# RWKV-7 recurrence hops: the old state is decayed and added on VectorE in place of identity matmuls, and each hop's output products stand behind the next hop's first products

## The chip, the cores and the metric

The kernel runs on one core of one Trainium2 chip. TensorE multiplies 128x128 tiles into PSUM, VectorE and ScalarE work on SBUF and PSUM, GpSimd (POOL) on SBUF; SyncE issues most of the transfers. The metric is the device time of one execution in microseconds, lower is better.

## The reference, cut to what matters

One layer of a bidirectional RWKV-7 / neighbourhood-attention network over 512 sample tokens and 128 prompt tokens, width 1024. The change lies in the RWKV branch, which has 8 heads of 64 channels and runs one recurrence forward and one backward:

```python
def _wkv_step(s, inp):
    r, w, k, v, a, b = inp
    sa = jnp.einsum("bhvk,bhk->bhv", s, a)
    s = s * w[:, :, None, :] + sa[..., None] * b[:, :, None, :] + v[..., None] * k[:, :, None, :]
    return s, jnp.einsum("bhvk,bhk->bhv", s, r)
...
    s_f, y_f = _wkv_scan(s0[:, 0], rh, _heads(decay[:, :, 0]), _heads(k_dir[:, :, 0]), vh,
                         -kk, kk * _heads(iclr[:, :, 0]), False)
    s_b, y_b = _wkv_scan(s0[:, 1], rh, _heads(decay[:, :, 1]), _heads(k_dir[:, :, 1]), vh,
                         -kk, kk * _heads(iclr[:, :, 1]), True)
    y = y_f + y_b
```

Around it stand the input projection, a gated merge with the attention branch, and a feed-forward block. The sample starts from a given state, the prompt from zero, and the prompt's last state is an output.

## The kernel before, in words

All is in fp32; the wide projections split each operand into a high and a low fp32r part and multiply three times (helpers at L223, L311 and L1856).

The recurrence is computed in chunks of 64 tokens. The sample gives eight chunks (slots `sl` 0 to 7), the prompt two (slots 8 and 9). Two heads, h = 0 and 1, share a tile of 128 partitions, one in each half, so four tiles `ct` are worked through one after the other. For each tile, `main` and `inv` form all products inside the chunks (tiles `AG`, `TG`, `R_`, `Rt`), and `carry` then hops from chunk to chunk with the state. A *line* `l` is a slot in one direction; a hop takes the forward and the backward line of a slot, so four products (two lines, two heads) make a group. Hops 0 and 1 also take the prompt's slots, and their groups have eight.

`ZV` holds for each line and head the incoming state in the head's own half of the partitions and the values in the other half. A hop `s` in the program's order:

1. First products (L1393), `AG` by `ZV`, into PSUM; ScalarE copies them to `x0` (L1396).
2. Identity products (L1405): the old state is multiplied by an identity matrix into the PSUM tile `pn`, so that the new state can be accumulated onto it. Not for slot 7, which has no successor, nor for slot 8, whose state is zero.
3. Old-state output products (L1411), `ZV` by `R_`, into the output tile `Y`.
4. Second products (L1420), `Rt` by `x0`; ScalarE writes them into `ZV` over the old state (L1426).
5. State products (L1433), `TG` by `ZV`, onto `pn`; VectorE multiplies `pn` by the decay `Dt` into the state half of the next line of `ZV` (L1445, one instruction for each head and both lines), or into `zf` for the prompt's last state (L1439).
6. Output products (L1450), `ZV` by `TG`, into `Y`.

After the last hop ScalarE copies `Y` out (L1455); the prompt's output is copied after hop 1 (L1453).

The order on TensorE, VectorE, ScalarE and POOL is that in which the program is written (`tc.manual_schedule`). `carry` is a generator that yields after the steps 1 to 3, after step 4 and after step 6. At each yield `weave` puts other work in: filler matmuls of the wide projections (L223), in a number from the table `plan`, and pieces of another generator. In carries 0 to 2 that one is the preparation of the next tile (L645 to L751, with a scan on VectorE at L696, the activations L650 to L721 on ScalarE, and `last`, which forms the next `AG` at L1168 and `R_` at L1171 on VectorE; the next tile's first matmuls are L1189). In carry 3 it is the gating of the merged outputs (L1554, L1556 and L1579 on VectorE, L195 splitting weights). After step 6 the plan has mostly six fillers in carries 0 to 2 and four in carry 3. The preparation of a scale (L682, L684), the elementwise steps L723 to L742 and the chunk inverse (L1310, L1317) appear in the profile too.

## Time and profile before

| | |
|---|---|
| median of 3 runs | 1151.46 us (1148.97 to 1151.8) |
| the profiled execution | 1151.04 us, of which the span is 1149.3 us |
| granted TensorE clock | 0.995 |
| busy: TensorE, VectorE, ScalarE, POOL | 97%, 68%, 46%, 17% of the span |
| first products (L1393) of the four carries | 298.9 to 627.1 us from the span's start |
| TensorE waiting at L1393 for VectorE's L1445 | 0.7 us, 3 times |

Times in the profile are microseconds from the start of the span. A matmul in fp32 is recorded as two instructions, so a count of x8 in the trace is four products of the program. Durations of matmuls overlap; what one costs TensorE is seen from the distance between starts. In brackets behind a row stands how long the engine was idle before it and what ended that.

### The profile page before, as it was taken

The numbers are of one execution on the slowest core, as the hardware profiler recorded it, in microseconds if no ns is written. First come the engines' busy times: TensorE is split into PE (matmuls) and PEld (weight loads), VectorE is DVE, ScalarE is ACT, GpSimd is POOL, SyncE is SP. The second block draws the span as 40 slices with busy tenths as digits, with TensorE's granted clock in tenths as the row PEclk, the third lists the DMA queues.
The fourth block names the chain that finished last, engine by engine and source line by source line (L and its number), as shares of the span: only waits on it lengthen the run. The fifth ranks groups of instructions, "written<-read, shape, count | busy, mean of one in ns | idle before, by whom it ended". The sixth has DMA issues, their size and how long they took to land.

```text
span 1149.3 us, 26860 instructions
## 1 busy us (share of the span) xinstructions
PE 1117.0 (97%) x11160; PEld 990.9 (86%) x11160; DVE 777.8 (68%) x1641; ACT 533.7 (46%) x1052; POOL 195.1 (17%) x262
## 2 busy tenths in 40 slices
PE   6999999999999999999999999999999999999998
PEld 4688878799888888888898788999899989998997
DVE  4565465769558847936787846897478747874775
ACT  4444576665465665456443524654134413441340
POOL 1163244321101212120100421110101010101000
PEclk8999999999999999999999999999999999999999
DMA  9752677654433533343743872222212221232122
GB/s 340 261 113 91 199 277 236 198 153 125 107 75 86 148 85 93 96 119 86 254 122 105 265 213 72 92 93 93 91 56 92 94 90 55 92 97 88 55 91 94
DMA packets 60482, 149.16 MB, mean 130 GB/s; under 512 B 7460, under 2 KB 22436, under 8 KB 60360
## 3 DMA queue, kind: packets, MB, share of 16 engines
q1 hardware_dynamic: 54888, 131.16, 34.7%
q0 software_dynamic: 4032, 14.68, 6.5%
q10 hardware_dynamic: 1440, 1.59, 0.5%
q8 instruction: 88, 1.44, 0.5%
q14 instruction: 34, 0.28, 0.1%
HBM read 118.41 MB, written 14.32 MB: 115 GB/s over the span
## 4 chain that ended last, share of the span: by engine, by line
PE 74%; DVE 10%; issue 8%; ACT 4%; DMA 2%; POOL 1%; SPq 0%; ACTq 0%; DVEq 0%; POOLq 0%
PE acc L311 24%; PE f L1856 21%; PE fl L223 8%; PE mm L223 5%; PE psa L1044 1%; PE lg L959 1%; PE pt L988 1%; DVE RL L1321 1%; DVE pr L1317 1%; PE po L1006 1%; PE w L1420 1%; PE w L1393 1%; DMA o<-o_d 1%; PE w L1433 1%; DMA wlo<-wst 1%
## 5 line engine op out<-in xcount | busy, mean ns | idle before, releaser
L1856 PE MATMUL f<-t,whi 128*128 128x320 f32 x640 | 141.7, 310 | 0.2
L311 PE MATMUL acc<-whi,u 128*128 128x512 f32 (+1 forms) x448 | 136.1, 386 | 0.0
L1856 PE MATMUL f<-b,whi 128*128 128x320 f32 x608 | 135.0, 310 | 0.4 <-DVE b L212 0.4
L223 PE MATMUL fl<-h,whi 128*128 128x320 f32 x672 | 121.4, 321 | 0.0
L1856 PEld LDWEIGHTS f<-t,whi 128*128 128x128 f32 x640 | 106.8, 188 | 0.8 <-issue 0.4
L223 PEld LDWEIGHTS fl<-h,whi 128*128 128x128 f32 x672 | 102.1, 189 | 4.6
L192 ACT CAST whi<-wst 128x1024 fp32r<-128x1024 f32 (+1 forms) x77 | 79.3, 1033 | 52.2 <-PE acc L311 41.5
L1856 PEld LDWEIGHTS f<-b,whi 128*128 128x128 f32 x608 | 101.7, 188 | 1.1 <-issue 0.6
L1856 PE MATMUL f<-t,wlo 128*128 128x320 f32 x320 | 98.9, 309 | 0.0
L311 PEld LDWEIGHTS acc<-whi,u 128*128 128x128 f32 x448 | 83.5, 188 | 16.6
L1856 PE MATMUL f<-b,wlo 128*128 128x320 f32 x304 | 94.1, 309 | 0.0
L1909 ACT CAST whi<-ws 128x1024 fp32r<-128x1024 f32 x40 | 42.0, 1051 | 104.5 <-PE f L1856 45.6
L311 PE MATMUL acc<-wlo,u 128*128 128x512 f32 (+1 forms) x224 | 86.3, 385 | 0.0
L1923 POOL TENSOR_TENSOR ws<-wst 128x512 f32<-128x512 f32 x20 | 29.1, 1454 | 334.7 <-DVE wlo L1912 226.3
L195 DVE TENSOR_TENSOR wlo<-wst,whi 128x1024 fp32r<-128x1024 f32 (+2 forms) x57 | 60.1, 1066 | 30.6 <-ACT whi L192 30.0
L311 PE MATMUL acc<-whi,h 128*128 128x512 f32 x240 | 79.2, 404 | 0.8 <-DVE h L436 0.8
L1724 DVE SCALAR_TENSOR_TENSOR tt<-acc,G 128x512 f32<-128x512 f32 (+1 forms) x51 | 34.7, 680 | 59.0 <-PE acc L311 45.4
L223 PE MATMUL fl<-h,wlo 128*128 128x320 f32 x336 | 63.8, 322 | 0.0
L1909 ACT CAST whi<-wst 128x1024 fp32r<-128x1024 f32 (+1 forms) x48 | 41.3, 869 | 42.3 <-PE acc L311 25.1
L1856 PEld LDWEIGHTS f<-t,wlo 128*128 128x128 f32 x320 | 60.1, 188 | 0.0
L1912 DVE TENSOR_TENSOR wlo<-ws,whi 128x1024 fp32r<-128x1024 f32 x40 | 55.4, 1386 | 5.4 <-ACT whi L1909 5.4
L1445 DVE TENSOR_TENSOR ZV<-w,Dt 64x128 f32<-64x128 f32 x64 | 18.4, 288 | 58.5 <-PE w L1433 57.4
(342 smaller groups left out, 2533.2 us busy)
## 6 DMA issues: line engine op xcount, KB each, us to landing
wst<-in_w_dram SPq DMA_DIRECT2D x66, 512.0 KB
wst<-in_w_rw_dram SPq DMA_DIRECT2D x31, 512.0 KB
wlo<-wst POOLq DMA_DIRECT2D x28, 512.0 KB, 4.7
wa<-in_w_ada_dram SPq DMA_DIRECT2D x24, 512.0 KB
f<-in_w_ada_dram SPq DMA_DIRECT2D x16, 512.0 KB
wst<-in_w_qkv_dram SPq DMA_DIRECT2D x12, 512.0 KB
o<-o_d SPq DMA_DIRECT2D x14, 320.0 KB
x<-in_xs_dram SPq DMA_DIRECT2D x8, 512.0 KB
```

The source lines that it names most:

```text
L192: act.copy(hi[:, :n], st[:, :n])
L195: dve.tensor_tensor(out=lo[:, a:b], in0=st[:, a:b], in1=hi[:, a:b].bitcast(F32), op=ALU.subtract)
L223: pe.matmul(ps[:, :t1 - t0], w[:, a:a + 128], x[:, k0 + kt, t0:t1], start=n == 0, stop=n == 3 * nk - 1)
L311: pe.matmul(pss[i][:, a:b], lhs(x, kt, ts_), w[:, cs_], start=ki == 0 and n == 0, stop=ki == last and n == 2)
L959: pe.matmul(psl[:, hd, o_:o_ + n], qT[ft][rows, qs], x[rows, :], start=True, stop=True)
L988: pe.transpose(pst[:, c * 128:(c + 1) * 128], L[:, c * 128:(c + 1) * 128], ident)
L1445: dve.tensor_tensor(out=V(ZV[own, l + 1, h, :], [[128 * dl, 2], [1, 64]]), in0=V(pn[own, :], [[64, 2], [1, 64]], 64 * g), in1=V(Dt[own, 0, ...
L1724: dve.scalar_tensor_tensor(out=tt, in0=ps[:, a:b], scalar=c, in1=G[:, g, sl], op0=ALU.mult, op1=ALU.mult)
L1856: pe.matmul(ps[:, :H2], w_[:, c_], x_[:, kt, :], start=first and kt + n == 0, stop=last and kt == 3 and n == 2, skip_group_check=more)
L1909: act.copy(r[0][:, :width], src())
L1912: dve.tensor_tensor(out=r[1][:, :width], in0=src(), in1=r[0][:, :width].bitcast(F32), op=ALU.subtract)
L1923: eng_x(PRM["se"][i - 1]).tensor_tensor(out=o_, in0=x, in1=y, op=op)
```

## The change

Three edits in `carry`, in every hop of the sample's slots (line numbers in the next two parts are those of the changed file):

- The identity products go, except for slot 9. In their place VectorE multiplies the old state by the decay into a new tile `sd` (L1381, one instruction a head), right after it has written that state and before step 4 overwrites it, and forms the new state as `pn` times decay plus `sd` (L1468, a scalar_tensor_tensor, one for each line and head, four in a hop). Slot 8 keeps its two multiplications (L1476).
- The output products of a hop move behind the first products of the next hop (`ysum`, L1388); those of the last hop stay at its end. The copy of the prompt's output moves with them.
- `x0` has one buffer in place of two.

```diff
+            sd = sb.tile([P, 2, 64], F32, tag="sd", bufs=1, name=nm("sd"))
+            begun, back = [], []
+            def decayed(l):
+                for h in range(2):
+                    own = hrows[h]
+                    dve.tensor_tensor(out=sd[own, :, :], in0=V(ZV[own, l, h, :], [[128 * 12, 2], [1, 64]]),
+                                      in1=V(Dt[own, 0, :], [[12, 2], [0, 64]], l), op=ALU.mult)
+            def ysum(items):
+                for (sl, d, l) in items:
+                    for h in range(2):
+                        pe.matmul(V(Y[sl // 8][hrows[h], :], *ycol(sl, d)), ZV[:, l, h, :], TG[:, l, h, 1, :],
+                                  start=once(Y[sl // 8], h), stop=sl in (7, 9) and d == 1)
...
-                x0 = sb.tile([P, 4, 64], F32, tag="x0", bufs=2, name=nm("x0"))
+                x0 = sb.tile([P, 4, 64], F32, tag="x0", bufs=1, name=nm("x0"))
                 act.copy(x0[:, :ng, :], V(px[:, :], [[64, ng], [1, 64]]))
+                if back:
+                    ysum(back)
+                    if s == 2:
+                        act.copy(y[:, 512:640], Y[1][:, 0:128])
...
-                            if sl != 8:
+                            if sl == 9:
                                 own = hrows[h]
                                 pe.matmul(pn[own, g * 64:g * 64 + 64], idh(h), ZV[own, l, h, :],
                                           start=once(pn, h), stop=False)
...
+                if s == 0:
+                    decayed(0)
...
+                        if sl < 8:
+                            for e in range(2):
+                                for h in range(2):
+                                    own = hrows[h]
+                                    dve.scalar_tensor_tensor(
+                                        out=ZV[own, l + 12 * e + 1, h, :],
+                                        in0=pn[own, (g + e) * 64:(g + e) * 64 + 64],
+                                        scalar=V(Dt[own, 0, :], [[1, 1]], l + 12 * e),
+                                        in1=sd[own, e, :], op0=ALU.mult, op1=ALU.add)
+                            continue
...
-                for (sl, d, l) in items:
-                    for h in range(2):
-                        pe.matmul(V(Y[sl // 8][hrows[h], :], *ycol(sl, d)), ZV[:, l, h, :], TG[:, l, h, 1, :],
-                                  start=once(Y[sl // 8], h), stop=sl in (7, 9) and d == 1)
-                if s == 1:
-                    act.copy(y[:, 512:640], Y[1][:, 0:128])
+                if s < 6:
+                    decayed(s + 1)
+                back = items
+                if s == 7:
+                    ysum(items)
                 yield
```

TensorE in the fourth carry, from the state products of hop 3 to the second products of hop 4. Before (L1433 state, L1450 output, L223 fillers, L1393 first, L1405 identity, L1411 old-state output, L1420 second products):

```order
L1433 MATMUL w_8666<-ZV,TG 64x64 x4
L1450 MATMUL w_8438<-TG,ZV 64x64 x4
L223 MATMUL fl_8683<-o_7947,whi_8295 128x320
L223 MATMUL fl_8683<-o_7943,wlo_8296 128x320 x2
L223 MATMUL fl_8683<-o_7944,wlo_8296 128x320
L1393 MATMUL w_8711<-ZV,AG 64x64 x4
L1405 MATMUL w_8718<-ZV,K 64x64 x4
L1411 MATMUL w_8438<-R__2901,ZV 64x64 x4
L1420 MATMUL w_8727<-x_1134_8716,Rt 64x64 x4
```

The same place now (L1454 state, L1408 first, L1388 output, L1430 old-state output, L1441 second products):

```order
L1454 MATMUL w_8672<-ZV,TG 64x64 x4
L223 MATMUL fl_8685<-o_7950,whi_8298 128x320
L223 MATMUL fl_8685<-o_7946,wlo_8299 128x320 x2
L223 MATMUL fl_8685<-o_7947,wlo_8299 128x320
L1408 MATMUL w_8713<-ZV,AG 64x64 x4
L1388 MATMUL w_8441<-TG,ZV 64x64 x4
L1430 MATMUL w_8441<-R__2901,ZV 64x64 x4
L1441 MATMUL w_8729<-x_1138_8718,Rt 64x64 x4
```

The output products have taken the place of the identity products, and only the four fillers still stand between state products and first products.

VectorE at the same place, from the state update of hop 2 to that of hop 3. Before (L1445 update, L1554 and L1556 gating of a projection, L1579 gating of the attention part):

```order
L1445 TENSOR_TENSOR ZV<-w_8608,Dt_6879 64x2x64 x2
L1554 SCALAR_TENSOR_TENSOR mx_8293<-mx_8293,fl_8563 128x320
L1556 TENSOR_TENSOR mt_7728<-mt_7728,mx_8293 128x320
L1579 SCALAR_TENSOR_TENSOR mt_8036<-pre_8486,mt_8036 128x320 x2
L1579 SCALAR_TENSOR_TENSOR P_1063_8081<-pre_8567,P_1063_8081 128x320 x2
L1445 TENSOR_TENSOR ZV<-w_8666,Dt_6879 64x2x64 x2
```

Now (L1468 update, L1381 decayed state for the hop after, L1584, L1586 and L1609 the same gating as before):

```order
L1468 SCALAR_TENSOR_TENSOR ZV<-w_8614,Dt_6880,sd_8443 64x64 x4
L1381 TENSOR_TENSOR sd_8443<-ZV,Dt_6880 64x128 x2
L1584 SCALAR_TENSOR_TENSOR mx_8296<-mx_8296,fl_8565 128x320
L1586 TENSOR_TENSOR mt_7731<-mt_7731,mx_8296 128x320
L1609 SCALAR_TENSOR_TENSOR mt_8039<-pre_8488,mt_8039 128x320 x2
L1609 SCALAR_TENSOR_TENSOR P_1066_8084<-pre_8569,P_1066_8084 128x320 x2
L1468 SCALAR_TENSOR_TENSOR ZV<-w_8672,Dt_6880,sd_8443 64x64 x4
```

Two instructions have become six, all ahead of the gating, and the gating keeps its place ahead of the next update.

1 line of the change is left out of this document (removed).

## The prediction

> **What bounds the kernel now.** I read the page first, then the timeline of the four carries (298.9 to 629.7 us), then windows of single hops, and last the rows that price an operation.
>
> ```profile
> span 1149.3 us, 26860 instructions
> PE 1117.0 (97%) x11160; PEld 990.9 (86%) x11160; DVE 777.8 (68%) x1641; ACT 533.7 (46%) x1052; POOL 195.1 (17%) x262
> L1445 DVE TENSOR_TENSOR ZV<-w,Dt 64x128 f32<-64x128 f32 x64 | 18.4, 288 | 58.5 <-PE w L1433 57.4
> ```
>
> TensorE is busy for 97% of the span, so work taken from it should count. VectorE at 68% looks free, and before the state update L1445 it sat idle 58.5 us in 64 updates, nearly all of it waiting for the state products L1433. Both are means over very different stages. The change touches only the hops, so I look there. This is one hop of the fourth carry, from its state update at 614.85 to the next at 618.57 (start, length, engine, line, operation; in brackets the idle time before it):
>
> ```profile
> 614.85 0.61 DVE L1445 TENSOR_TENSOR ZV<-w,Dt 64x128 f32<-64x128 f32 x2 [0.46 <-PE w L1433]
> 615.49 0.49 DVE L1554 SCALAR_TENSOR_TENSOR mx<-mx,fl 128x320 f32<-128x320 f32 x1
> 615.75 0.45 PE L1393 MATMUL w<-ZV,AG 128*64 128x64 f32 x8
> 616.13 0.45 PE L1405 MATMUL w<-ZV,K 64*64 64x64 f32 x8
> 616.41 0.40 PE L1411 MATMUL w<-R__2901,ZV 64*64 64x64 f32 x8
> 616.42 0.89 DVE L1579 SCALAR_TENSOR_TENSOR P<-pre,P 128x320 f32<-128x320 f32 x2
> ...
> 617.74 0.49 DVE L1556 TENSOR_TENSOR mt<-mt,mx 128x320 f32<-128x320 f32 x1
> 618.07 0.45 PE L1433 MATMUL w<-ZV,TG 128*64 128x64 f32 x8
> 618.35 0.40 PE L1450 MATMUL w<-TG,ZV 128*64 128x64 f32 x8
> 618.57 0.61 DVE L1445 TENSOR_TENSOR ZV<-w,Dt 64x128 f32<-64x128 f32 x2 [0.34 <-PE w L1433]
> 618.68 0.71 PE L223 MATMUL fl<-o,wlo 128*128 128x320 f32 x3
> 619.47 0.45 PE L1393 MATMUL w<-ZV,AG 128*64 128x64 f32 x8
> ```
>
> TensorE never pauses in it, and VectorE works without a break from 615.49 to 618.23 (the left-out line is another L1554) and has 0.34 us to spare out of 3.72. The windows from one state update of this carry to the next say the same (columns: length, then busy time of PE, PEld, DVE, ACT, POOL):
>
> ```profile
> 602.07:607.17 5.10, 5.10 (x114) 4.51 (x110) 3.18 (x8) 1.87 (x7) 0.00 (x0) 1.00 0.13 36
> 607.17:611.13 3.96, 3.96 (x74) 3.37 (x68) 2.63 (x7) 2.01 (x6) 0.00 (x0) 1.00 0.19 64
> 611.13:614.85 3.72, 3.72 (x66) 3.13 (x60) 3.16 (x9) 0.79 (x3) 0.00 (x0) 1.00 0.69 204
> 614.85:618.57 3.72, 3.72 (x66) 3.13 (x60) 3.25 (x9) 0.79 (x3) 0.00 (x0) 1.00 0.48 146
> 618.57:622.29 3.72, 3.72 (x66) 3.13 (x60) 3.25 (x9) 1.62 (x4) 0.00 (x0) 1.00 0.05 19
> 622.29:626.01 3.72, 3.72 (x66) 3.13 (x60) 2.52 (x6) 0.79 (x3) 0.00 (x0) 1.00 0.62 165
> ```
>
> Three hops hold 3.16 to 3.25 us of VectorE work in 3.72 us. Here the engine that the change loads is almost as full as the one that it relieves, and its queue is in a fixed order.
>
> **The change part by part: what it removes.** Identity products go for the sample's slots: four in each of seven hops, 28 in a carry, 112 in all; four in a carry stay, for the prompt. Their price is the pitch on TensorE. In the hop above four of them take 616.41 - 616.13 = 0.28 us; eight of them, in hop 1 of the first carry:
>
> ```profile
> 307.37 0.68 PE L1405 MATMUL w<-ZV,K 64*64 64x64 f32 x16
> 307.89 0.63 PE L1411 MATMUL w<-R__2901,ZV 64*64 64x64 f32 x16
> ```
>
> That is 0.52 us. So one costs (0.52 - 0.28) / 4 = 0.06 us, and 0.04 is the change of operand shape, which stays. 112 x 0.06 = 6.7 us is all that TensorE can gain, 0.24 in a hop. In hop 0 of each carry the second products wait for ScalarE's copy of the first ones, and no older output products fill that place, so I credit nothing there: 24 x 0.24 = 5.8 us at most.
>
> **What it adds to VectorE.** In a hop two multiplications of 64x128 become four fused ones of 64x64 and two 64x128 multiplications into sd for the hop after. No run here has the fused form, so I bound it by neighbours:
>
> ```profile
> 602.07 1.25 DVE L1445 TENSOR_TENSOR ZV<-w,Dt 64x128 f32<-64x128 f32 x4 [3.16 <-PE w L1433]
> L684 DVE SCALAR_TENSOR_TENSOR kk<-kt__626,C,w x3: 340/340/342, 313.9 to 511.1; 128x128 f32<-128x128 f32 x3
> 585.02 1.16 DVE L1310 SCALAR_TENSOR_TENSOR RL<-RL 128x28 f32<-128x28 f32 x6
> L1317 DVE TENSOR_TENSOR pr<-RL 128x126 f32<-128x126 f32 x8 | 2.2, 274 | 0.0
> L1168 DVE TENSOR_TENSOR AG<-kk,P x16: 806/821/825, 244.9 to 541.2; 64x640 f32<-64x640 f32 x16
> 438.41 3.37 DVE L1168 TENSOR_TENSOR AG<-kk,P 64x640 f32<-64x640 f32 x4
> 441.81 1.56 DVE L1171 TENSOR_TENSOR R__2901<-rt__625,P 128x640 f32<-128x640 f32 x2
> ```
>
> A fused operation with a scalar per partition and one input in PSUM takes 340 ns at 128 elements (L684) against 288 for L1445. An element costs 1.06 ns (L1168 821 at 640 elements, L1317 274 at 126), so 64 elements fewer make about 272 ns. How closely the operations follow each other matters as much. L1171, of the same length as L1168, covers all partitions, and its second one starts 1.56 - 0.82 = 0.74 us after the first; L1168 alternates between the two halves of the partitions and stands at (3.37 - 0.82) / 3 = 0.85, with no overlap at all. L1445 alternates too: (1.25 - 0.29) / 3 = 0.32. The new operations alternate in the same way, so I take duration plus 0.03: 0.30 us each. The ends are L1310, which doesn't alternate, 1.16 / 6 = 0.19, and L684's full length, 0.37; the alternation makes the upper half the nearer one. The two into sd cost 0.274 + 0.03 = 0.30 each (L1317).
>
> [...]
>
> So a hop gives VectorE 4 x 0.30 + 2 x 0.30 = 1.80 us instead of 2 x 0.32 = 0.64: +1.16. The last state update of a carry has no multiplication behind it: +0.56. In all about 28 us of new work.
>
> **What that does to the chain.** From the state products at 618.07 the update starts 0.50 later, and the next first products stand 0.90 behind that, at 619.47; 0.28 to 0.33 of this was the output products' time, which now lie elsewhere. So the cover is some 0.6 us, with 0.17 more until the fourth first product. The four updates need 3 x 0.30 + 0.27 + 0.04 = 1.21. Behind four filler products, as in this carry, TensorE waits about 0.4 in every hop even with an idle VectorE, more than the 0.24 gained. With six, as in the other carries, 0.3 more stands before them and the wait is about 0.1.
>
> *Fourth carry.* Hop 0: the prompt's two multiplications now end 0.56 later, and the first products of hop 1 end with them; behind these stand eight output products that ran in their shadow before. TensorE is 0.5 us late after hop 1. From hop 2 on VectorE's own work decides: update start plus 1.80 plus the other work of that hop (615.49 to 618.23 is 2.74; by the windows 2.62 for the hop before, 2.74 for the one after, 2.00 for the last). Starts were 611.13, 614.85, 618.57, 622.29, 626.01; they become 611.65, 616.07, 620.61, 625.15, 628.95. Late at the end: 2.9, and with 0.56 more in the last update less what TensorE gained, **+3.0 us**. The outputs of this carry feed the last projection directly, so it stays.
>
> *Third carry.* Here VectorE has room, but the recurrence shares it with the next tile's preparation:
>
> ```profile
> 511.36 0.60 DVE L1445 TENSOR_TENSOR ZV<-w,Dt 64x128 f32<-64x128 f32 x2
> 512.52 1.49 DVE L696 TENSOR_TENSOR_SCAN pre<-K,pre 128x640 f32<-128x640 f32 x1
> 514.10 0.83 ACT L702 ACTIVATE P<-pre 128x320 f32<-128x320 f32 x2
> 516.17 1.36 ACT L653 ACTIVATE pre<-w,D 128x320 f32<-128x320 f32 x3 [0.26 <-PE w L647]
> 517.41 0.27 ACT L1396 COPY x<-w 128x128 f32<-128x128 f32 x1
> 530.03 0.83 DVE L742 TENSOR_TENSOR f<-NK,pre 128x640 f32<-128x640 f32 x1
> 530.96 0.65 ACT L721 ACTIVATE NK<-pre,D 128x320 f32<-128x320 f32 x1 [1.61 <-DVE f L742]
> 531.81 0.45 PE L1420 MATMUL w<-x,Rt 64*64 64x64 f32 x8 [0.39 <-ACT x L1396]
> ```
>
> The scan L696 stands behind update and sd: +1.16, less 0.34 that TensorE had gained by then (two hops, less waits of 0.1), +0.8. ScalarE takes L702 and all behind it in order, its idle 0.26 before L653 goes, and its copy x0 at 517.41, for which TensorE waits, comes 0.5 late. In the hops after that gain and waits cancel. At the end L742 stands behind the last update: 0.5 + 0.56, and L721, the copy and L1420 behind it: **+1.05**.
>
> *Second and first carry.* The same pattern, estimated in the same way: the scan 0.45 and 0.25 late, then the last update 0.56, less 0.2 to 0.4 that TensorE had gained: **+0.75** and **+0.4**. In the second the AG rows (438.41, ending 441.78) run into the next stage's first products, so it is passed on. In the first:
>
> ```profile
> 339.91 1.20 ACT L721 ACTIVATE NK<-pre,D 128x320 f32<-128x320 f32 x2 [0.60 <-DVE f L742]
> 341.31 0.73 PE L1450 MATMUL w<-TG,ZV 128*64 128x64 f32 x8 [0.71 <-ACT ZV L1426]
> ```
>
> the carry's last output products wait for a ScalarE queue that waits for VectorE, so what TensorE gained is lost there.
>
> Other edits: x0 with one buffer costs nothing, since its writer already waits for products that stand behind the reader. The output copy L1453 moves behind one x0 copy, which is a gain if anything. On SP a weight load passes the state loads of the next carry, which are needed a whole stage later.
>
> Sum: 3.0 + 1.05 + 0.75 + 0.4 = **+5.2 us**, in which the 5.8 us of TensorE are already spent. The profiled execution took 1151.04 us (span 1149.3 and 1.7 around it), 0.4 below the median of 1151.46; on the median it is **1156.6 us**.
>
> **The rivals.**
> - *The gain arrives.* If the fused operations overlap as L1310 does (0.19) the updates end 0.8 us after their start and six fillers cover them, the scans move little, and carries one to three keep 18 x 0.24 = 4.3 us. The fourth then needs about 3.25 + 4 x 0.19 + 0.60 - 0.64 = 4.0 us a hop and loses near 0.5. Net -3.8: 1147.7 us, faster. For it: 97% on TensorE, 58.5 us idle at L1445. Against it: the alternation of L1168. It decides below a pitch of about 0.2. Chance 0.12.
> - *Half and half.* Pitch 0.25, if the fused form costs no more than a multiplication (L1445's 288 less 64 x 1.06 is 220 ns, and 0.03 between): the fourth carry loses 1.9, the third 0.65, the second 0.35, the first nothing: +2.8, 1154.3 us. [...] Against it: L684. Chance 0.26.
> - *Worse.* Pitch 0.37: 0.28 more in each of 28 updates, of which the fourth carry passes on 1.5 and the others 0.4 each: +8, 1159.5 us. Chance 0.14.
> - That the change does not remove what it says is out: the order of instructions shows the 112 gone.
>
> **How the numbers follow.** My forecast, with chance 0.48, is 1156.6 us. A measurement of this kernel can tell about 0.3% from no change, here 1148.0 to 1154.9. The first rival is faster, the second within, mine and the third slower: 0.12, 0.26, 0.62. The range leaves out the faster case and the far end of the third: 1150.5 to 1161.5 us.
>
> **What would show it.** In the profile after: the fused row at about 270 ns, and four of them in about 1.2 us; first products waiting for ZV of VectorE in most hops, 0.7 us in all before, then several us; hops of the fourth carry of 4.4 us in place of 3.72, with VectorE full; L696 and the last L742 of carries two and three later behind ZV. I am wrong if four fused ones take under 0.9 us, or if the fourth carry isn't the longest to grow.

## The result, and the profile after

The changed kernel takes 1164.99 us (median of six runs, 1162.23 to 1167.67), the kernel before beside it 1151.12; the ratio is 1.0122, 95% interval 1.0100 to 1.0143. So it is 13.9 us slower, where 1156.6 us was forecast (at most 1161.5). The profiled execution is the slowest of the six, 1167.67 us. From its page, the rows that answer to those of before:

```profile
span 1165.9 us, 26548 instructions
PE 1125.2 (97%) x10936; PEld 993.4 (85%) x10936; DVE 810.4 (70%) x1753; ACT 535.5 (46%) x1052; POOL 194.0 (17%) x262
L1468 DVE SCALAR_TENSOR_TENSOR ZV<-w,Dt,sd 64x64 f32<-64x64 f32 x112 | 31.6, 283 | 46.4 <-PE w L1454 43.4
```

VectorE has 32.6 us more work (28 were forecast, with six pairs of multiplications into sd in a carry; the code has seven, x56 in all), and TensorE is still busy for 97%, but now of 16.6 us more. TensorE lost 224 product records and as many weight loads for 112 products: a product in fp32 shows as two weight loads and two products, so it is four instructions. That will matter.

Where the time went is read from one mark in both traces: the start of a hop's first products (L1393 before, L1408 after). The windows run from hop 0 to hop 7 of a carry, and from there to hop 0 of the next one. First before, then after (ends, length, busy time of PE, PEld, DVE, ACT, POOL, granted clock, DMA share, GB/s):

```profile
298.86:337.23 38.37, 37.69 (x549) 32.97 (x548) 12.78 (x29) 23.38 (x62) 4.48 (x8) 1.00 0.30 76
337.23:394.22 56.99, 55.34 (x1082) 51.11 (x1082) 52.56 (x161) 33.32 (x66) 11.57 (x22) 1.00 0.44 112
394.22:433.19 38.97, 37.45 (x545) 32.62 (x544) 17.11 (x35) 23.43 (x62) 4.54 (x8) 1.00 0.34 94
433.19:492.36 59.17, 56.12 (x1086) 51.64 (x1085) 51.87 (x161) 33.01 (x65) 12.84 (x22) 1.00 0.38 99
492.36:530.59 38.23, 37.50 (x547) 32.91 (x546) 14.26 (x31) 22.77 (x61) 5.79 (x9) 1.00 0.42 110
530.59:598.49 67.90, 64.68 (x1148) 59.88 (x1147) 54.71 (x164) 33.40 (x68) 7.34 (x13) 1.00 0.50 166
598.49:626.91 28.42, 28.42 (x488) 24.31 (x487) 19.25 (x47) 9.89 (x31) 0.00 (x0) 1.00 0.40 121
```

```profile
296.91:337.99 41.08, 38.31 (x485) 33.06 (x485) 22.70 (x60) 23.78 (x62) 5.11 (x9) 0.96 0.28 73
337.99:400.87 62.88, 58.28 (x1090) 53.43 (x1090) 55.37 (x168) 33.33 (x66) 11.58 (x22) 0.97 0.41 106
400.87:440.11 39.24, 37.50 (x482) 32.43 (x481) 21.38 (x57) 23.86 (x62) 4.18 (x8) 0.96 0.32 87
440.11:499.05 58.94, 56.46 (x1095) 52.05 (x1094) 52.41 (x161) 33.06 (x65) 13.47 (x23) 1.00 0.39 102
499.05:538.82 39.77, 37.37 (x483) 32.04 (x482) 22.23 (x59) 22.92 (x61) 5.04 (x8) 1.00 0.38 102
538.82:611.27 72.45, 66.92 (x1156) 61.69 (x1155) 55.73 (x165) 33.51 (x68) 7.34 (x13) 0.98 0.48 155
611.27:643.09 31.82, 31.39 (x423) 24.80 (x423) 26.05 (x72) 10.09 (x31) 0.00 (x0) 1.00 0.33 98
```

The fourth carry grows by 3.4 us and the third by 1.5, as foreseen in kind. But the two longest growths, 5.9 and 4.55 us, lie **between** carries one and two and carries three and four, in stages whose code was not touched and whose products are those of before, but for hop 6's output products, which now stand behind hop 7's first ones (x1090 and x1156 against x1082 and x1148). In them TensorE stands still where it waits for no semaphore. Three rows of its timeline ("issue" means that the profile shows nothing that it waited for; such a wait is called one without a releaser below):

```profile
355.71 0.28 PE L1211 MATMUL w<-R__2901,f 64*64 64x64 f32 x3 [1.50 <-issue]
...
384.60 0.21 PE L1208 MATMUL w<-AG,f 64*64 64x64 f32 x1 [1.51 <-issue]
...
577.25 0.21 PE L1211 MATMUL w<-R__2901,f 64*64 64x64 f32 x1 [2.01 <-issue]
```

Before, the same stages had 0.42 us of this, while the stage between carries two and three had a wait of 1.52, where 0.52 is left after. Two more rows fit them. In the queue list of the page, instructions arrive by DMA in packets of 16 KB (packets, MB, share of 16 engines). Before:

```profile
q8 instruction: 88, 1.44, 0.5%
```

After:

```profile
q8 instruction: 86, 1.41, 0.5%
```

TensorE's 22,320 and 21,872 weight loads and products make 254 for each packet in both; with the semaphore instructions of its queue they are 22,508 and 22,057, 256 for each. So, as an estimate from these counts, a packet of 16,384 bytes holds 256 instructions of 64 bytes, and the queue looks like TensorE's own. The DMA view of 353.2 to 354.3 and that of 381.6 to 383.2 us show one such packet each; they have landed as the first two waits begin, at 354.2 and 383.1, some 1.4 us before these end. The experiments below come back to this.

And TensorE's clock is halved in four stretches of 3.41 us, at 305.36, 356.56, 407.76 and 578.43 (half-clock windows from here on; those at the start and the end of the program, which both kernels have, are left out); before there was one, at 294.6. Two of them with the window ahead of each:

```profile
353.15:356.56 3.41, 1.91 (x58) 1.53 (x53) 3.30 (x9) 1.41 (x7) 0.75 (x6) 1.00 0.52 155
356.56:359.98 3.42, 3.42 (x14) 3.35 (x13) 2.57 (x12) 0.62 (x2) 0.00 (x0) 0.50 0.15 53
575.02:578.43 3.41, 1.40 (x26) 1.04 (x21) 0.00 (x0) 0.00 (x0) 0.00 (x0) 1.00 0.17 64
578.43:581.84 3.41, 3.41 (x13) 3.01 (x12) 3.37 (x13) 1.06 (x3) 0.86 (x1) 0.50 0.00 0
```

By the granted clock of 0.50 over 3.41 us each costs, as an estimate, up to half its length, 1.7 us, where TensorE sets the pace.

### The profile page after: what moved, and what is told of

Same layout as the page of the kernel before. It is cut to its first block, busy times and chain, and to the rows that moved or that the text cites. A ratio compares the mean times of both kernels' runs of the same rounds, so it can differ in the third digit from the quotient of the medians.

```text
span 1165.9 us, 26548 instructions
## 1 busy us (share of the span) xinstructions
PE 1125.2 (97%) x10936; PEld 993.4 (85%) x10936; DVE 810.4 (70%) x1753; ACT 535.5 (46%) x1052; POOL 194.0 (17%) x262
## 4 chain that ended last, share of the span: by engine, by line
PE 71%; DVE 12%; issue 9%; ACT 5%; DMA 2%; POOL 1%; SPq 0%; ACTq 0%; DVEq 0%; POOLq 0%
PE acc L311 24%; PE f L1886 21%; PE fl L223 8%; PE mm L223 5%; DVE RL L1321 1%; DVE pr L1317 1%; PE pt L988 1%; PE lg L959 1%; PE po L1006 1%; PE psa L1044 1%; PE w L1408 1%; PE w L1441 1%; ACT whi L192 1%; DMA o<-o_d 1%; DMA wlo<-wst 1%
## 5 line engine op out<-in xcount | busy, mean ns | idle before, releaser
L223 PE MATMUL fl<-h,whi 128*128 128x320 f32 x672 | 121.6, 321 | 0.0
L223 PEld LDWEIGHTS fl<-h,whi 128*128 128x128 f32 x672 | 102.2, 190 | 4.6
L311 PEld LDWEIGHTS acc<-whi,u 128*128 128x128 f32 x448 | 83.5, 188 | 16.6
L1468 DVE SCALAR_TENSOR_TENSOR ZV<-w,Dt,sd 64x64 f32<-64x64 f32 x112 | 31.6, 283 | 46.4 <-PE w L1454 43.4
L223 PE MATMUL fl<-h,wlo 128*128 128x320 f32 x336 | 63.5, 320 | 0.2 <-issue 0.2
```

The source lines that it names most:

```text
L223: pe.matmul(ps[:, :t1 - t0], w[:, a:a + 128], x[:, k0 + kt, t0:t1], start=n == 0, stop=n == 3 * nk - 1)
L311: pe.matmul(pss[i][:, a:b], lhs(x, kt, ts_), w[:, cs_], start=ki == 0 and n == 0, stop=ki == last and n == 2)
L1468: dve.scalar_tensor_tensor(out=ZV[own, l + 12 * e + 1, h, :], in0=pn[own, (g + e) * 64:(g + e) * 64 + 64], scalar=V(Dt[own, 0, :], [[1, 1] ...
```

## The experiments

Three theories. **A**: the hops cost what was forecast, nearly, and the rest is TensorE waiting for its next block of 256 instructions, in stretches of short products that use a block up faster than the next one arrives; which stretch a border between two blocks hits depends on how many instructions stand ahead, and the change took 112 out of each carry. **B**: the state loads, which a weight load passes on SyncE's queue, delay something there. **C**: half-clock windows follow stretches that the change thinned out.

Several runs add idle products, whose results nothing reads. Where the texts on record price one at 0.03 us and two instructions, read 0.06 us and four. This is the timeline's row of 100 of them, in count_shift_before:

```profile
295.88 6.05 PE L1394 MATMUL w<-ZV,K 64*64 64x64 f32 x200
```

So 28 cost 1.7 us of TensorE and make 112 instructions. The shifts aimed at come out the same, since what they replace is counted wrongly by the same factor.

The table gives the growth against the trace of before in us, by the starts of first products as above: ahead of the first carry, then carries (c) and stages between them (s), then the rest. The half-clock window of before at 294.6 lies in "ahead", so -1.7 there is no gain. "Median" is against the median of before in the same comparison.

```
run                    ahead   c1    s1    c2    s2    c3    s3    c4   rest  median
after                  -1.9  +2.7  +5.9  +0.3  -0.2  +1.5  +4.5  +3.4  +0.5  +13.9
after_again            -1.8  +2.4  +4.1  -1.3  -0.3  +1.1  +4.9  +3.4  +2.2  one run
replace_only           -2.6  +1.0  +5.8  -1.5  -0.5  +1.6  +3.6  +3.0  +0.3  +10.7
move_only              -0.9  +2.7   0.0  +0.1  +0.1  -0.3  +1.6  +0.1  +4.1   +7.4
restore_count          -0.8  +1.3  +2.2  +0.3  +2.8  +0.3  +3.1  +3.4  +0.9  +13.1
same_half_first        -1.2  +0.4  +3.6  -1.7  -0.5  +1.2  +3.0  +2.0  +0.3  +11.1
count_shift_before     +3.0   0.0  +4.7  -1.4  -0.3   0.0  +2.0   0.0   0.0   +9.0
fourth_as_before       -3.2  +2.7  +6.2  +0.2  -0.3  +1.1  +3.6   0.0  +0.4  +13.0
halves_gpsimd_fourth   -2.2  +2.2  +3.3  -0.3  -0.5  +1.2  +3.3  +1.1  +0.8   +9.8
idle_in_gap            -2.6  +2.1  +0.4  +0.9  +0.9  +2.3  +2.6  +3.4  +0.5  +12.0
all_repairs            -2.9  +1.7  +0.5  +0.5  +0.6  +1.9  +3.2  +1.1  +0.9  +10.7
first_two_only         -2.9  +1.7  +0.5  +0.4  +0.2  +0.1  -0.3   0.0   0.0   +2.6
hop0_unmoved           -0.7  +0.6  +4.4  -1.7  -0.3  +1.9  +3.6  +2.9  +6.2  +15.7
early_28               +5.7  +1.3  +1.2  +1.6  +0.7  +3.7  +1.0  +3.4  +0.5  +18.7
early_56               +2.1  -0.1  +2.4  -0.4  +1.0  +0.5  +9.3  +3.4  +0.5  +18.3
early_84               +6.9  -0.2  +1.3  +1.2  +0.5  +3.7  +3.3  +3.4  +0.5  +20.7
before_16              -2.3  +0.7  +0.7   0.0  -1.0  +0.5  +0.3   0.0   0.0   -0.6
before_32              -0.9   0.0  +0.2   0.0  -1.1  +0.6  +1.3   0.0   0.0   -0.9
before_48              -0.1   0.0  +1.0   0.0  -1.1  +0.5  +4.1   0.0   0.0   +4.7
```

**The two halves of the change.** One kernel leaves the output products in place (`ysum(items)` at the end of the same hop, no `back`), the other keeps identity products and multiplications (`if sl != 8:` in place of `if sl == 9:`, no `decayed`, no fused form).

> The change without its second half: VectorE adds the decayed old state, the output products stand where they stood before. TensorE's instruction count and the four more VectorE operations per hop are those of the full change; SyncE's queue is in the order of the kernel before. Theory A (the hops cost about 6.6 us, and the rest of the loss is TensorE waiting for blocks of its own instruction stream between the carries, whose places depend on how many instructions stand before them, and half-clock windows behind such waits): 1161 to 1167 us, and waits of TensorE with no releaser of 1.5 to 2 us in the stages between the carries, as in the changed kernel. Theory B (weight loads that pass the state loads on SyncE's queue delay something between the carries): that order is not changed here, so only the hops' cost is left, 1155 to 1159 us. By the prediction on record, 1156 to 1158 us.

> The other half alone: the output products stand behind the next hop's first products, the identity products and the two state multiplications stay. TensorE's instruction count and SyncE's order are those of the kernel before. The multiplications end 0.64 us after the state products, with some 0.6 us of cover, and the output products lie under ScalarE's copy x0. Theory A and theory B both expect nothing between the carries and at most 0.1 us per hop: 1150 to 1154 us. If moving the output products is itself what takes the cover from the update, 0.3 us in each of 28 hops: about 1159 us.

Measured: 1161.80 us (ratio 1.0097, 1.0078 to 1.0116) and 1158.48 (1.0060, 1.0044 to 1.0075). With SyncE's queue as before, replace_only has the waits of the changed kernel and grows by 5.8 us between the first carries: theory B falls. move_only keeps the count and has no growth there (0.0), and the hops of its second, third and fourth carry cost at most 0.1 us; the first grows by 2.7, of which a half-clock window can make 1.7. Yet it is 7.4 us slower. 1.6 of that lie in the last stage between carries, with a half-clock window, and 4.1 far behind the recurrence, in a half-clock window at 686 us and in this row of TensorE's timeline:

```profile
685.20 0.50 PE L311 MATMUL acc<-wlo,m 128*128 128x512 f32 x1 [2.57 <-DMA wlo<-wst]
```

That wait was 0.6 us before. Why this weight copy comes later there stays open, and the expected 1150 to 1154 us was missed.

**The count put back, at a price** (the code shortened).

```
+ if s == 0:                      # head of carries one to three
+     for j in range(28): pe.matmul(px[own, 0:64], idh(j % 2), ZV[own, 0, j % 2, :], ...)
```

> The changed kernel with 28 idle 64x64 products at the head of each of the first three carries, so that the stages between the carries begin at the same number of TensorE instructions as in the kernel before. Each costs about 0.03 us, 2.5 us in all. Theory A: the waits of 1.5, 1.5 and 2.0 us between the carries go back to the 0.4 to 1.5 us of before, and the half-clock windows behind them go too, so 1157 to 1162 us in spite of the added products, and the starts of the second and fourth carry are no longer 5.6 and 3.7 us further behind than the ends of the carries ahead of them. Theory B: SyncE's order is unchanged from the changed kernel, so nothing goes away and the products are added: 1166 to 1169 us.

Measured: 1164.26 us (1.0109, 1.0092 to 1.0126), beyond the 1157 to 1162 expected. But the idle products cost 1.7 us in three places, 5.1 in all, and the changed kernel plus 5.1 would be 1170. The first stage between carries grew by 2.2, of which 1.7 are idle products, where the changed kernel has 5.9; neither of its two waits of 1.5 us is there. The wait near 475 us is back (1.8), as in the kernel before.

**The count shifted in the kernel before** (100 idle products ahead of the first carry, 28 ahead of the second).

> The kernel before with nothing of the change: 100 idle 64x64 products at the head of the first carry and 28 at the head of the second. The 200 instructions of the first (a weight load and a product each) put the blocks of 256 where they lie in the changed kernel while the stage between the first and second carry runs (256 less 56), and the 56 of the second bring them back to where they lay before. Price of the idle products 0.03 us each, 3.8 us in all. Theory A (the place of the block borders makes the waits): in that stage two waits of TensorE of about 1.5 us each without a releaser appear, at the same products as in the changed kernel, the second carry starts 4 to 6 us later beyond the 3 us, and the later stages are as before: 1157 to 1161 us. Theory B (what waits there comes from the hops, or from the order on SyncE's queue): no such waits, 1154 to 1156 us.

Measured: 1159.41 us (1.0078, 1.0064 to 1.0093). With nothing of the change in it, the waits stand at the products where the changed kernel has them:

```profile
357.20 0.28 PE L1211 MATMUL w<-R__2901,f 64*64 64x64 f32 x3 [1.38 <-issue]
...
383.88 0.21 PE L1208 MATMUL w<-AG,f 64*64 64x64 f32 x1 [1.24 <-issue]
```

The stage grows by 4.7 us, 1.7 of them idle products. The first, third and fourth carry are as before to 0.0 us. The second gains 1.4 us without any change in its hops, and all of it in hop 0: before, TensorE waited there 0.78 us for VectorE's L1364, and a TensorE that comes later doesn't. So part of what the stage loses comes back, and the gains in that column are not the change's doing. The last stage between carries grows by 2.0, with a wait of 0.73 without a releaser, where nothing was expected. The 128 idle products can account for up to 7.7 of the 9.0 us, so in this kernel the moved borders alone cost little in the end: 3.0 - 1.4 - 0.3 + 2.0 = 3.3 us by the stages, at least 1.3 by the median.

**A second trace of the changed kernel.**

> The changed kernel once more, for a second trace. Theory A: the waits of TensorE without a releaser stand at the same instructions (0.9 us near 255, 1.5 near 354, 1.5 near 383, 0.5 near 495, 2.0 near 575), since the count of instructions ahead of them is fixed; the half-clock windows may lie elsewhere, since their grid of 3.41 us has another phase in each execution, but behind thin stretches: the heads of the first and second carry and the waits named. Rival: the waits wander as well.

```profile
355.32 0.28 PE L1211 MATMUL w<-R__2901,f 64*64 64x64 f32 x3 [1.30 <-issue]
...
382.63 0.21 PE L1208 MATMUL w<-AG,f 64*64 64x64 f32 x1 [1.51 <-issue]
...
573.54 0.21 PE L1211 MATMUL w<-R__2901,f 64*64 64x64 f32 x1 [1.93 <-issue]
```

The same three instructions, as expected: these waits belong to the program. Half-clock windows stand again at 305 and 575 us, the second behind the wait of 1.93 us that ends at 573.54; those at 357 and 408 are gone, and one at 667 us is new. The grid that the expectation speaks of is seen in the first trace: its four windows start 51.20, 51.20 and 170.67 us apart, 15, 15 and 50 lengths of a window, and the one of before, at 294.61, lies 0.5 us off that grid.

**The order of the fused operations** (`for h in range(2): for e in range(2):`, outer and inner loop exchanged).

> The changed kernel with the four fused operations in another order: both of the lower half of the partitions first, then both of the upper half, instead of alternating; nothing else is changed. The prediction put the pitch of 0.30 us down to the alternation. If that is right, the two that follow in the same half stand 0.19 to 0.25 us apart, the group of four is 0.1 to 0.2 us shorter, and with 28 groups of which some half are waited for the time falls by 1 to 3 us. If the length of the operation alone sets the pitch, it stays at 0.31 us and nothing changes (within 1 us).

Measured: 1162.21 us (1.0092, 1.0072 to 1.0111), 2.8 us under the changed kernel, though the two intervals overlap. A group of four on VectorE's timeline, in the changed kernel:

```profile
629.36 1.22 DVE L1468 SCALAR_TENSOR_TENSOR ZV<-w,Dt,sd 64x64 f32<-64x64 f32 x4
```

and here:

```profile
624.89 0.99 DVE L1468 SCALAR_TENSOR_TENSOR ZV<-w,Dt,sd 64x64 f32<-64x64 f32 x4
```

With three changes of half the pitch is (1.22 - 0.29) / 3 = 0.31 us; with one it averages (0.99 - 0.29) / 3 = 0.23, by the starts 0.20 within a half and 0.30 across. The alternation costs 0.1 us each time, and the fourth carry shrinks by 1.4. This is read from the traces and doesn't hang on the medians.

**The fourth carry alone** (`ct < 3` at each edit), and then **with GpSimd** (by halves, and `(pool if ct == 3 else dve)` for the two multiplications into sd).

> The changed kernel with its first three carries changed and the fourth as in the kernel before. By the prediction on record the fourth carry alone costs 3.0 us, by the trace of the changed kernel 3.9 us. Theory A: the hops of the fourth carry go back to 3.72 us, the start of the fourth carry stays as late as in the changed kernel, and 3 to 4 us go: 1161 to 1162 us. Rival: what the fourth carry loses was hidden anyway behind the weight loads of the next stage, less than 1 us goes.

> The changed kernel with the fused operations ordered by halves, and in the fourth carry alone the two multiplications into sd on GpSimd, which has nothing to do there. VectorE then has in a hop of that carry four fused operations (0.99 us) in place of 1.80, its other work is 2.6 to 2.7 us: 3.7 us, as long as a hop of the kernel before. If VectorE's fullness is what lengthens the fourth carry, it loses at most 1 us (2.2 us with the order by halves alone, 3.9 in the changed kernel) and the time is 1160 to 1161.5 us. If GpSimd takes over 1.5 us for the pair, or slows VectorE's operations beside it, the fourth carry stays at 2 to 4 us.

Measured: 1163.46 us (1.0112, 1.0097 to 1.0127) and 1160.27 (1.0080, 1.0068 to 1.0093). The first missed its 1161 to 1162: its fourth carry is back at 0.0 us, and the 3.4 us don't turn up behind it ("rest" is +0.4), but against the kernel before the median fell only from +13.9 to +13.0, as the rival had it, and its profiled execution has four half-clock windows in mid-run. The second came out nearly as expected: the fourth carry grows by 1.1 us (at most 1 was expected) in place of 2.0 (by halves) and 3.4, since GpSimd takes the pair off a full engine and has it done, at 624.27 in the row below, 2.3 us before the next update at 626.55:

```profile
623.34 0.93 POOL L1381 TENSOR_TENSOR sd<-ZV,Dt 64x128 f32<-64x128 f32 x2 [2.89 <-DVE ZV L1468]
```

**The thinned stretch.** In hop 0 the old output products stood ahead of a wait for ScalarE (L664, 0.42 and 0.23 us before in the first two carries, 0.87 and 0.71 after); theory C puts the half-clock windows at 305 and 408 us down to the stretch left thinner there. One kernel fills this place with the 28 idle products, one leaves the output products of hop 0 there (`if s in (0, 7): ysum(items)`).

> The changed kernel with 28 idle 64x64 products at the end of hop 0 of the first three carries, where the output products stood before they were moved. They restore the count of instructions, as in the experiment on the count, but here they stand ahead of a wait for ScalarE (0.87 and 0.71 us in the first two carries), so they should cost little. [...] Filled again, both windows go: with the waits between the carries gone too, 1156 to 1160 us and a mean clock of 0.997 or more. Rival: the half-clock windows there are chance or come from something else: 1161 to 1163 us at the clock of the changed kernel, 0.994.

> The changed kernel with the output products of hop 0 of each carry left where they stood before, ahead of the wait for ScalarE behind that hop; those of the other hops are moved. The count of instructions at the end of each carry is that of the changed kernel, so the waits between the carries stay. Theory C: the head of the first and second carry is filled again, no half-clock window at about 305 and 408 us, and 1.5 to 3 us go: 1162 to 1163.5 us. Rival, after the idle products that removed these two windows in one trace and left the mean clock at 0.995: as the changed kernel, 1164 to 1166 us.

Measured: 1162.60 us (1.0097, 1.0081 to 1.0114) and 1166.00 (1.0128, 1.0111 to 1.0145). In both traces the half-clock windows at 305 and 408 us are gone (in the 3.41 us ahead of them TensorE was busy for 2.54 and 2.70 us in the changed kernel; with the idle products it is busy for all 3.42 us from 301.58 on), and with hop 0 unmoved the first carry grows by 0.6 us in place of 2.7, of which the window can make 1.7. But the times and mean clocks of the first (0.992 to 0.997 in its six runs) go by the rival, and the second loses the gain, and more, in a wait of 4.2 us for the weight copy that move_only waited for. Theory C explains single windows; that it moves the median isn't shown. The first does confirm A once more: its first stage between carries grows by 0.4 us.

**All repairs, and the change in two carries only.**

> All that the experiments name, together: the changed kernel with the fused operations ordered by halves, the multiplications into sd on GpSimd in the fourth carry, and the 28 idle products at the end of hop 0 of the first three carries. If the losses add up, the hops cost 0.6 - 1.4 + 1.8 + 1.4 = 2.4 us over the kernel before, the waits between the carries are those of before, and the clock is that of before: 1152 to 1155 us. If the half-clock windows stay: 1156 to 1158 us.

> The change in the first two carries alone, by halves, with the 28 idle products in those two; the third and fourth carry are as in the kernel before. The hops of the first carry cost 0.6 us, those of the second gain 1.4, nothing else differs from the kernel before: 1149.5 to 1152 us, the version that could come out level or a little faster. If half-clock windows at the heads of the two carries stay, 1153 to 1154 us.

Measured: 1161.28 us (1.0083, 1.0067 to 1.0099) and 1153.24 (1.0019, 1.0006 to 1.0031). Both miss; the second lies where it was put with half-clock windows at the heads of the carries, but its trace has none. The idle products, 1.85 us in the first carry, fill a wait of 0.87, so part of what the repairs save is spent on them, and half-clock windows remain (one at 564 us in the first one's trace). What the second kernel would take without its two such groups was not measured.

**Idle products where they cost nothing.** TensorE waits 6.6 us for its first weights; 28 idle 16x16 products end there at 2.8 us, 84 at 5.8.

```
+ for j in range(28):             # 56, 84; and 4, 8, 12 in the kernel before
+     pe.matmul(psa[0:16, 0:16], mhalf[:, 0:16], mhalf[:, 0:16], start=True, stop=True)
```

> The changed kernel with 28 idle 16x16 products at the very start, in the 6.6 us in which TensorE waits for its first weights (they read a constant and write PSUM columns that are cleared afterwards). A product in fp32 is two passes, each a weight load and a product, so 112 instructions go ahead of everything, as many as a carry has lost: the stage between the first and second carry then begins at the count of the kernel before, the later ones at counts that no run has had. Theory A: in that stage the waits of 1.5 and 1.5 us go and it is 57 to 58 us long in place of 61 to 63, the later stages may gain or lose; time 1158 to 1162 us. If the place of the blocks is worth little: 1164 to 1166 us.

> The same with 56 idle products, 224 instructions: now the stage between the second and third carry stands at the count of the kernel before. Theory A: its wait of 1.5 us comes back (near 475 us), the other two stages are at new counts; time between 1158 and 1167 us, and the sum of the waits without a releaser accounts for the difference from the other two within 2 us.

> The same with 84 idle products, 336 instructions: the stage between the third and fourth carry stands at the count of the kernel before. Theory A: its wait of 2 us goes and the stage is 69 to 71 us long in place of 72.5; the other two are at new counts; time 1158 to 1166 us, again with the sum of the waits.

Measured: 1170.23, 1169.80 and 1172.20 us (1.0162, 1.0144 to 1.0179; 1.0160, 1.0143 to 1.0176; 1.0179, 1.0162 to 1.0196). The places came out nearly as named: with 28 the first stage is 58.2 us long; with 56 the wait at 475 returns; with 84 the last stage has no such wait and is 71.2 us long. The times did not. With 28 and 84 I had left out the stage ahead of the first carry, whose borders move too (+5.7 and +6.9); with 56 the last stage between carries grows by 9.3, with waits of 2.30 and 2.64 us and three half-clock windows. The longest waits of early_28:

```profile
286.52 0.27 PE L1213 MATMUL w<-R__2929,f 64*64 64x64 f32 x2 [3.68 <-issue]
```

of early_56:

```profile
259.21 0.42 PE L1191 MATMUL w<-AG,f 64*32 64x64 f32 x5 [3.69 <-issue]
...
480.92 0.21 PE L1210 MATMUL w<-AG,f 64*64 64x64 f32 x1 [1.53 <-issue]
...
599.33 0.27 PE L1250 MATMUL w<-ZV,J 64*64 64x64 f32 x2 [2.64 <-issue]
```

and of early_84:

```profile
288.04 0.33 PE L1213 MATMUL w<-R__2985,f 64*64 64x64 f32 x3 [3.46 <-issue]
```

The fourth carry grows by 3.4 us in all of them. The sum of the waits does not account for the differences within 2 us, as it was expected to; half-clock windows come on top.

> The kernel before with nothing of the change, and 4 idle products (16 instructions) at the very start, while TensorE waits for its first weights. Theory A: all block borders come 16 instructions earlier in the program; the waits without a releaser stay in the same stages (the stage ahead of the first carry, and that between the second and third, 1.5 us near 475), each by up to some tenths of a us longer or shorter: 1150 to 1154 us, carries as before. If the kernel before is by chance at the best place, every shift is slower.

> The same with 8 idle products, 32 instructions: 1149 to 1156 us, the difference from before accounted for by the waits without a releaser and the half-clock windows within 2 us; the carries as before.

> The same with 12 idle products, 48 instructions: nearer to the shift of 80 of the run with 84 products, in which the stage ahead of the first carry had waits of 2.1 and 3.5 us; 1150 to 1159 us, the carries as before.

Measured: 1150.64 us (1.0000, 0.9989 to 1.0010), 1150.36 (0.9994, 0.9983 to 1.0004) and 1155.94 (1.0050, 1.0031 to 1.0068). Twelve idle products in a place where nothing waits for them make the kernel before 4.7 us slower; its carries are as before to 0.5 us, and these waits are new or longer:

```profile
284.78 1.18 PE L223 MATMUL fl<-h,whi 128*128 128x320 f32 x7 [1.81 <-issue]
...
351.43 0.56 PE L223 MATMUL fl<-h,whi 128*128 128x320 f32 x2 [1.38 <-issue]
...
591.48 0.71 PE L223 MATMUL fl<-o,whi 128*128 128x320 f32 x3 [1.42 <-issue]
```

So the kernel before stands at a good place, and no kernel here is measurably faster than it.

**Where in the stream the waits stand.** If all records of TensorE's queue in a trace (weight loads, products, semaphore instructions) are numbered from 0 by their starts, theory A can be read off directly. Some of the waits of 0.4 us and more without a releaser, with the number of the record that ends the wait, and how many packets of q8 had begun by then:

```
run                  ends at   wait  line    record  =  blocks    packets
before                351.81   0.42  L1259     7106  =  27*256+194   27
after                 355.71   1.50  L1211     7106  =  27*256+194   27
before_48             351.43   1.38  L223      7106  =  27*256+194   27
count_shift_before    357.20   1.38  L1211     7618  =  29*256+194   29
after                 384.60   1.51  L1208     8129  =  31*256+193   31
count_shift_before    383.88   1.24  L1208     8641  =  33*256+193   33
after                 577.25   2.01  L1211    14017  =  54*256+193   54
early_56              599.33   2.64  L1250    14785  =  57*256+193   57
```

The same holds for all 83 such waits of the 20 traces, 0.42 to 3.69 us long: each ends at record 193 or 194 of a block of 256, whatever the instruction is, as many packets have begun as whole blocks lie ahead of it, and the last of them landed 1.16 to 1.61 us before. None of the 424 waits of that length that have a releaser stands there. Most borders are passed without a wait (the changed kernel has 86 packets and 5 such waits), also many behind blocks that TensorE ran through as fast: in the changed kernel the blocks ahead of the five waits took it 1.3 to 4.6 us, and eight others of 1.3 to 4.6 us end in no such wait. What decides between these is open.

## Why the prediction was wrong, point by point

- **The direction** (slower) was right, and so is the sum for the hops, but with its parts shifted. Hop 0 of a carry moves with the moment at which TensorE gets there, also with nothing of the change in the kernel (+0.7 in the first carry of before_16, -1.4 in the second of count_shift_before, +0.5 in the third of before_48). So the hops are read from hop 1's first products to hop 7's, in traces without a half-clock window there. The first carry shows -0.1 to +0.1 us (replace_only, idle_in_gap, early_56), the second 0.1 (after_again), the third 0.9, the fourth 3.9 (its hop 0 gives back 0.5, and what follows it adds 0.5). The forecast was 0.4, 0.75, 1.05 and 3.0. What the first two carries were to lose comes only behind their hop 7, where it was foreseen: the last output products wait 1.06 us for ScalarE in place of 0.71, and the next tile's first matmuls wait for `AG`, which they did not before:

```profile
342.69 0.73 PE L1388 MATMUL w<-TG,ZV 128*64 128x64 f32 x8 [1.06 <-ACT ZV L1447]
...
449.58 0.83 PE L1189 MATMUL w<-AG,f 64*32 64x64 f32 x64 [0.56 <-DVE AG L1168]
```

With these the hops cost some 6 us for 5.2. That the sum comes so near is in part luck: the first two carries lose less than was forecast in their hops, and the fourth more.

- **The third carry** ends as worked out: L742 behind the update, and TensorE waiting for x0 behind it, 0.81 us in place of 0.39:

```profile
537.86 1.23 DVE L1468 SCALAR_TENSOR_TENSOR ZV<-w,Dt,sd 64x64 f32<-64x64 f32 x4
539.12 0.82 DVE L742 TENSOR_TENSOR f<-NK,pre 128x640 f32<-128x640 f32 x1
...
540.90 0.45 PE L1441 MATMUL w<-x,Rt 64*64 64x64 f32 x8 [0.81 <-ACT x L1411]
```

- **The fused operation**: 283 ns for 272 forecast, pitch 0.31 for 0.30, four in 1.22 us for 1.2; the operations into sd 289 ns each for 274. That the alternation sets the pitch is now shown by exchanging two loops: 0.20 us within a half, 0.30 across. L1168 beside L1171 (0.85 us against 0.74) had pointed the right way; the second rival's 220 ns for an operation did not fit the fused form.
- **The fourth carry** went as worked out. VectorE's queue sets the pace, pitches 4.42, 4.54, 4.54 and 3.80 us forecast, measured 4.43, 4.55, 4.55 and 3.97. The 0.9 us above the forecast lie mostly at the start: counted from the start of the carry, hop 2's update comes 1.0 us later than before, not 0.5. Two of these hops, from update to update:

```profile
624.93:629.36 4.43, 4.43 (x54) 3.61 (x54) 4.21 (x12) 0.78 (x3) 0.00 (x0) 1.00 0.49 166
629.36:633.92 4.56, 4.50 (x52) 3.36 (x51) 4.30 (x14) 0.79 (x3) 0.00 (x0) 1.00 0.36 106
```

- **The wait that takes the removed one's place** is there: first products (L1408) wait for VectorE's ZV 20 times, 4.8 us in all, for 0.7 before. Not foreseen: ScalarE's write of ZV (L1447) waits twice for the multiplications into sd, 4.4 us of ScalarE's time, both in a hop 0.
- **The step that failed** is "what it removes". It priced 112 identity products at 112 x 0.06 = 6.7 us and took that for all that their removal does to TensorE. The price was right (100 idle ones took 6.05), but the removal also moves every later instruction against the borders of TensorE's blocks, in stages that the change does not touch, and these stages were put at nothing. They lose 5.9 + 4.55 - 0.2 = 10.2 us in one trace and 8.7 us in the other. Of the 10.2, waits without a releaser make 3.5 (5.8 after, 2.3 before), the two half-clock windows up to 3.4, longer waits for VectorE and ScalarE 1.4 (among them the 0.56 above), and hop 6's output products, which moved there out of the carries, 0.8; some 1.1 are not accounted for. 1.4 us come back in hop 0 of the second carry. Neither the sum nor a rival had a term for these stages but the waits for VectorE and ScalarE, so the range was too narrow. The rows that hinted at it were at hand: waits of TensorE with no releaser, 0.4 to 1.5 us, stood in the trace of before.
- **The clock**: the mean granted clock was 0.994 over the six runs of the changed kernel (0.991 to 0.996) and 0.997 over the 77 of the kernel before beside the experiments (0.994 to 1.000), which is 0.003 x 1165 = 3.5 us if TensorE sets the pace all the time. The prediction had no term for this either. Some of these windows follow the waits above, some the thinned hop 0, but not each time. In the second trace of the changed kernel the wait at 382.63 lies in a window in which TensorE is as little busy as in that at 353.15 above, and the clock behind it stays full:

```profile
380.40:383.82 3.42, 1.91 (x66) 1.71 (x55) 3.28 (x17) 3.40 (x6) 0.00 (x0) 1.00 0.27 103
383.82:387.23 3.41, 3.41 (x25) 3.41 (x24) 3.34 (x12) 0.75 (x2) 1.01 (x3) 1.00 0.21 43
```

So what halves the clock is not settled here, and with it some 3 us of the loss.

That a border of blocks makes these waits is shown by shifting the count (count_shift_before, early_*, before_48), by putting it back, and by the place of all 83 in the stream. That what TensorE lacks there is the next packet of instructions is an inference of mine from the packets' kind, their number (88 and 86) and their landing 1.16 to 1.61 us before a wait ends; what TensorE does in those last 1.16 to 1.61 us no run shows. How much of the 13.9 us the borders make is known less well: 3.5 us of waits in one trace, less what comes back behind them, and the half-clock windows only as far as they follow from the waits.

## What to carry to other kernels

In this kernel, where TensorE runs hundreds of short products in a row, the number of instructions ahead of them was itself a parameter worth several us: 12 idle products at the start made the kernel before 4.7 us slower. Before a small change is judged on such a kernel, look for waits without a releaser in both traces, and shift the count by some idle products at a place where TensorE waits anyway; a difference that moves with them is not the change's. And where VectorE's operations alternate between the halves of the partitions, try them grouped by half: four took 0.99 us here in place of 1.22.

## What the hardware showed that was not expected

- TensorE stops for 0.4 to 3.7 us where the profile shows nothing that it waits for, in all 83 cases of the 20 traces at record 193 or 194 of a block of 256 of its queue, and in both traces of the changed kernel at the same instructions.
- In the four half-clock windows of the changed kernel's first trace the clock is halved (0.50) for 3.41 us after a window of the same length in which TensorE was busy for 1.40 to 2.70 us. The windows ahead of those at 356.56 and 578.43 were not idle (1.91 and 1.40 us busy): they hold a stretch of short products and a wait of 1.5 to 2 us. Such a window isn't always followed by half rate: in the second trace, behind the one at 380.40 with 1.91 us busy, the clock is 1.00.
- One operation on GpSimd of 64x128 takes 0.40 us in the median where VectorE takes 0.29, and beside it VectorE's fused ones take 0.99 to 1.13 us for four (0.99 to 1.00 without it).
